# Prompt attention's compressed scores moved apart and cut in column quarters, and four smaller moves, in a one-core hybrid decoder layer

## The chip, the cores and the metric

The kernel runs on one core of one Trainium2 chip. The metric is the device time of one execution, in microseconds; lower is better. Three executions of the kernel before gave 1314.0, 1316.9 and 1320.02 us, so the median is 1316.9 us.

## The reference, cut to what matters

One layer of a decoder, in fp32, for a prompt of 256 tokens and 8 samples of 8 tokens (320 tokens together), with half a feed-forward step on either side:

```
x = x + 0.5 * SwiGLU1(RMSNorm(x))
P = RMSNorm(x) @ w_in_proj           # z, xBC, dt | q, k/v x 3, gates | merge gates
y_ssd = mamba_mixer(z, xBC, dt, ...)      # causal conv, chunked scan, gated norm
y_nsa = gates[0] * o_c + gates[1] * o_s + gates[2] * o_w
x = x + (sig(gA) * (y_ssd @ w_branch_ssm) + sig(gB) * (y_nsa @ w_branch_attn)) @ w_out
x = x + 0.5 * SwiGLU2(RMSNorm(x))
```

`o_c` is attention over compressed keys, one for each block of 32 rows; `o_s` over the 16 best of the blocks of 64 rows, where the ranks come from the sums of the compressed probabilities; `o_w` over a window of 512. For the prompt all blocks fit among the 16, so only the samples rank. Sample queries also see a cache of 2048 rows in pages. The change touches the prompt's part of `o_c`, the samples' ranks, the loads ahead of the samples' attention, and the evacuations behind two of the last projections.

## The kernel before, in words

**Dense stream.** All big products go through `dense()`: an fp32 weight block of 128x1024 is loaded by SyncE (`w_load`, L308), split by ScalarE into a rounded part `wh` (`w_hi`, L317) and by VectorE into the rest `wl` (`w_lo`, L326), and for each of 8 chunks TensorE runs three matmuls of 128x128 by 128x320 (L345 to L347). There are three raw buffers, and a new load is asked for behind `w_lo`, which is given out behind the third chunk of a unit. The order of every engine's queue is the order in which the Python code calls.

**Side work.** Attention, the scan and their preparations are Python generators. After each chunk `S.tick()` may run a step of them (`S.step()`), so their instructions stand between the dense ones on each engine. `yield` ends a step, `wait(n)` lets n of them pass, and `S.defer(n, f)` calls f some n dense units later. Two chains run side by side: prompt_attn, then the scan (`ssd`), then sample_attn; and prompt_cmp, values_tok, new_keys, cmp_sample. During the prompt's attention the dense units are those of xBC, each of which also gives a convolution: `taps` (three VectorE operations, L1245, then a tanh on ScalarE, L1246) and `gate` (L1249, L1252).

**PSUM.** Banks are taken in rings by kind: `pd` (3, dense results), `sc` (2), `pt` (2), `po` (1). A matmul into a bank waits until the bank's last use has been read out.

**The places the change touches.** `values_tok` turns the values over in two halves t (L1035, L1041). In prompt_attn, for each quarter qc of 64 queries, `build` (GpSimd, L1281) writes the queries of a pair of heads into a zeroed matrix, `cmp_a` multiplies it with the compressed keys `kTp` (8 matmuls, L1288) and runs a softmax on VectorE and ScalarE (L1293 to L1303), and `cmp_b` turns four heads of the result (L1310) and copies them out by ScalarE (L1311). The 32 pairs of scores go through `scores` (L1317, L1323, L1326), `norm` (L1334, L1337), `transposes` (L1349, L1350) and `values` (L1366). In `cmp_sample` two matrices U of 30x30 comparisons are made by VectorE (L1169), masked by GpSimd (L1170) and summed by VectorE (L1174, L1175). `early_bias` has SyncE load the samples' bias in 16 pieces (L1440) and the window mask `wb` (L1444), between two stages; sample_attn adds the two first (L1458). Behind the last steps stand the loop over `wbs` (the mixer's branch, `split` of yh and yl), the loop over `wba` and the loop over `wo` (out projection, L2070 to L2076), whose results x are scaled and split again (`norm_pre`: L416 on VectorE, L261 on ScalarE, L264 on VectorE) for the second feed-forward step.

Of the kernel before, what the change touches and what calls it, by code (L numbers as in the profile page):

```python
# [10 lines left out]
F32 = mybir.dt.float32  # L11
# [4 lines left out]
ALU = mybir.AluOpType  # L16
# [91 lines left out]
NST = 2  # L108
# [83 lines left out]
def wait(n):  # L192
    for _ in range(n):
        yield
# [3 lines left out]
def step_kernel(ctx, tc, I, O):  # L198
# [3 lines left out]
    S = Sched()  # L202
# [828 lines left out]
    def values_tok():  # L1031
        for t in range(2):
            pv = bank("pt")
            for i in range(4):
                pe.transpose(pv[:, 128 * i : 128 * i + 128], vr[:, i, 128 * t : 128 * t + 128], ident)  # L1035
            a.copy(flat(vtp[:, t]), pv)
            yield
        pv = bank("pt", (128, 256))
        for br in range(2):
            for h2 in range(2):  # L1040
                pe.matmul(pv[64 * br : 64 * br + 64, 128 * h2 : 128 * h2 + 128], vr[:, 2 * br + h2, 256:], ident,  # L1041
                          start=True, stop=True)
        a.copy(vst, pv)
        yield
# [85 lines left out]
    def cmp_sample():  # L1130
# [35 lines left out]
        for j in range(2):  # L1166
            sj = ib[:, j, 1:31].unsqueeze(1).to_broadcast([128, 30, 30])
            si = ib[:, j, 1:31].unsqueeze(2).to_broadcast([128, 30, 30])
            v.tensor_tensor(U[j], sj, si, op=ALU.is_gt)  # L1169
            g.tensor_tensor(U[j], U[j], um, op=ALU.mult)  # L1170
        yield from wait(4)
        cs = pq.tile([128, 2, 30], F32, name="rkc")
        for j in range(2):
            v.reduce_sum(rk[:, j, :], U[j], axis=AX.X)  # L1174
            v.reduce_sum(cs[:, j, :], U[j].rearrange("p i j -> p j i"), axis=AX.X)  # L1175
            yield from wait(2)
        v.tensor_tensor(rk, rk, cs, op=ALU.subtract)
# [83 lines left out]
    def prompt_attn():  # L1261
# [22 lines left out]
        def cmp_a(qc):  # L1284
            nb, k0 = 2 * (qc + 1), 192 - 64 * qc
            pc = bank("pt", (128, 8, 8))
            for u in range(8):
                pe.matmul(pc[:, u, :nb], qbp[qc % 2][:, u, :], kTp[:, u // 4, :nb], start=True, stop=True)  # L1288
            sc = pl.tile([128, 8, 8], F32, tag="psc", name="psc")
# [84 lines left out]
        build(0)  # L1374
        yield from wait(2)
        cmp_a(0)
        yield from wait(4)
        cmp_b(0, 0)
        cmp_b(0, 1)
        for i in range(4):  # L1380
            scores(i)
            yield
            if i:
                norm(i - 1)
        transposes(0)
        yield
        for i in range(32):
# [10 lines left out]
            if qc < 3:  # L1398
                if u == 1:
                    build(qc + 1)  # L1400
                elif u == 2:
                    cmp_a(qc + 1)
                elif u == 4:
                    cmp_b(qc + 1, 0)
                    cmp_b(qc + 1, 1)
            yield
# [26 lines left out]
    def early_bias(n):  # L1433
        pl = right.enter_context(tc.tile_pool(name="sb", bufs=1, side="right"))
        st["bias"] = pl.tile([128, PAST], F32, name="bias")
        for i in range(2 * T):
            t, s = divmod(i, 2)
# [3 lines left out]
            if i % n == n - 1:  # L1441
                yield
        st["wb"] = pl.tile([128, 8], F32, name="wb")
        sp.dma_start(st["wb"], I["wm"])  # L1444
        yield

# [587 lines left out]
    for h in range(2):  # L2034
# [4 lines left out]
        for k in range(8):  # L2039
            split(yh[:, k, :], yl[:, k, :], xbc[:, 8 * h + k, :])  # L2040
        for _ in range(NST):
            S.step()
        for m in range(8):
# [26 lines left out]
    for m in range(8):  # L2070
        p = bank("pd", (128, NT))
        dense(wo[m], mh, ml, p)
        v.scalar_tensor_tensor(x2[:, m, :], p, 0.5, x2[:, m, :], op0=ALU.mult, op1=ALU.add)  # L2073
        norm_pre(x2, m, P_N2, hh, hl)
        sq.add(x2[:, m, :])
    rsb = norm_scale(sq, so)  # L2076
# [157 lines left out]
```

## Time and profile before

| what | before |
|---|---|
| median of 3 executions | 1316.9 us |
| the profiled execution, its time | 1319.28 us |
| its span (first to last instruction) | 1317.6 us |
| mean granted TensorE clock | 0.981 |
| TensorE busy with matmuls | 1260.2 us (96%) |
| VectorE busy | 877.1 us (67%) |
| ScalarE busy | 590.5 us (45%) |
| GpSimd busy | 347.0 us (26%) |

The span is 1.7 us shorter than the execution's time. Busy times are of the whole span. The stages by the clock of the span: first feed-forward step up to 360 us; projections for attention 375 to 460; xBC with the prompt's attention beside it 460 to 660; merge gates, z and the scan 660 to 830; the samples' attention 840 to 996; wba and wo 1023 to 1076; second feed-forward step to the end. A granted clock of 1 is TensorE's upper level of 2.4 GHz, 0.5 the lower one of 1.2 GHz.

### The profile page before, as it was taken

The numbers are of one execution on the slowest core, as the hardware profiler recorded it, in microseconds if no ns is written. First come the engines' busy times: TensorE is split into PE (matmuls) and PEld (weight loads), VectorE is DVE, ScalarE is ACT, GpSimd is POOL, SyncE is SP. The second block draws the span as 40 slices with busy tenths as digits, with TensorE's granted clock in tenths as the row PEclk, the third lists the DMA queues.
The fourth block names the chain that finished last, engine by engine and source line by source line (L and its number), as shares of the span: only waits on it lengthen the run. The fifth ranks groups of instructions, "written<-read, shape, count | busy, mean of one in ns | idle before, by whom it ended". The sixth has DMA issues, their size and how long they took to land. (4 is left out here: it accounts for less than half of the span.)

```text
span 1317.6 us, 28585 instructions
## 1 busy us (share of the span) xinstructions
PE 1260.2 (96%) x10779; PEld 1151.3 (87%) x10779; DVE 877.1 (67%) x1872; ACT 590.5 (45%) x1149; POOL 347.0 (26%) x567
## 2 busy tenths in 40 slices
PE   8999999999999998889999998898999999999998
PEld 8999999999988888777897777775769999999998
DVE  5576666655586577976568888777678665656542
ACT  4444444444455334446664442455564343333322
POOL 2233221232200335655335664121210010000000
PEclk9899999999999998999999999898999999999999
DMA  8466666766663445521167876998974444444553
GB/s 275 146 215 213 206 197 197 233 202 221 203 195 121 138 147 212 189 69 50 65 207 236 269 228 194 325 339 289 331 284 154 152 145 135 146 154 150 153 163 92
DMA packets 102212, 251.67 MB, mean 191 GB/s; under 512 B 14648, under 2 KB 41273, under 8 KB 100121
## 3 DMA queue, kind: packets, MB, share of 16 engines
q1 hardware_dynamic: 89722, 213.44, 49.1%
q0 software_dynamic: 12352, 36.40, 8.4%
q8 instruction: 85, 1.39, 0.4%
q14 instruction: 53, 0.43, 0.1%
HBM read 235.07 MB, written 23.10 MB: 196 GB/s over the span
## 5 line engine op out<-in xcount | busy, mean ns | idle before, releaser
L345 PE MATMUL ps_pd<-hh,wh 128*128 128x320 f32 x1320 | 440.9, 334 | 2.9 <-ACT hh L261 1.8
L326 DVE TENSOR_TENSOR wl<-wraw,wh 128x1024 fp32r<-128x1024 f32 (+1 forms) x245 | 303.2, 1239 | 178.0 <-ACT wh L317 172.2
L346 PE MATMUL ps_pd<-hl,wh 128*128 128x320 f32 x1320 | 413.8, 314 | 1.3 <-DVE hl L454 1.1
L347 PE MATMUL ps_pd<-hh,wl 128*128 128x320 f32 x1320 | 413.7, 313 | 1.2 <-DVE wl L326 1.1
L317 ACT CAST wh<-wraw 128x1024 fp32r<-128x1024 f32 (+1 forms) x245 | 252.1, 1031 | 139.1 <-PE ps_pd L346 99.8
L345 PEld LDWEIGHTS ps_pd<-hh,wh 128*128 128x128 f32 x1320 | 253.2, 192 | 22.0 <-issue 11.4
L346 PEld LDWEIGHTS ps_pd<-hl,wh 128*128 128x128 f32 x1320 | 253.6, 192 | 9.5 <-issue 4.8
L347 PEld LDWEIGHTS ps_pd<-hh,wl 128*128 128x128 f32 x1320 | 253.0, 192 | 2.0 <-DVE wl L326 2.0
L345 PE MATMUL ps_pd<-ah,wh 128*128 128x320 f32 x352 | 109.4, 311 | 0.0
L347 PE MATMUL ps_pd<-ah,wl 128*128 128x320 f32 x352 | 108.9, 309 | 0.0
L580 DVE TENSOR_TENSOR pgl<-pg,pgh 128x512 fp32r<-128x512 f32 x128 | 82.5, 685 | 29.6 <-ACT pgh L573 29.3
L346 PE MATMUL ps_pd<-al,wh 128*128 128x320 f32 x320 | 98.8, 309 | 0.0
L568 POOL DMA_DIRECT2D pg<-in_cache x136 | 74.2, 546 | 83.6 <-DVE pgl L580 42.3
L238 POOL TENSOR_SCALAR ah<-ff 128x320 fp32r<-128x320 f32 x44 | 20.1, 457 | 275.0 <-DVE ff L482 275.0
L477 ACT ACTIVATE sg<-sg 128x320 f32<-128x320 f32 x44 | 20.8, 472 | 127.1 <-DVE sg L476 127.1
L573 ACT CAST pgh<-pg 128x512 fp32r<-128x512 f32 x128 | 72.7, 616 | 10.0 <-PE ps_sc L714 8.0
L713 PE MATMUL ps_sc<-pgh,w1h 128*128 128x256 f32 x256 | 68.5, 288 | 1.3 <-ACT pgh L573 1.3
L714 PE MATMUL ps_sc<-pgh,w1l 128*128 128x256 f32 x256 | 68.2, 288 | 0.0
L345 PEld LDWEIGHTS ps_pd<-ah,wh 128*128 128x128 f32 x352 | 66.2, 188 | 0.4
L347 PEld LDWEIGHTS ps_pd<-ah,wl 128*128 128x128 f32 x352 | 66.1, 188 | 0.0
L346 PEld LDWEIGHTS ps_pd<-al,wh 128*128 128x128 f32 x320 | 60.2, 188 | 0.0
L1431 POOL DMA_DIRECT2D KV<-in_cache x54 | 29.1, 539 | 109.4 <-PE ps_po L1526 90.6
(476 smaller groups left out, 2207.5 us busy)
## 6 DMA issues: line engine op xcount, KB each, us to landing
wraw<-in_wproj SPq DMA_DIRECT2D x77, 512.0 KB
wraw<-in_w1in SPq DMA_DIRECT2D x44, 512.0 KB
wraw<-in_w2in SPq DMA_DIRECT2D x44, 512.0 KB
pg<-in_cache POOLq DMA_DIRECT2D x136, 128.0 KB, 4.0
pg<-in_cache SPq DMA_DIRECT2D x120, 128.0 KB
KV<-in_cache POOLq DMA_DIRECT2D x54, 256.0 KB, 5.9
KV<-in_cache SPq DMA_DIRECT2D x54, 256.0 KB
wraw<-in_w1out SPq DMA_DIRECT2D x16, 512.0 KB
```

Source lines behind the costliest of these rows:

```text
L317: a.copy(h[:, :n], st["raw"][i][:, :n])
L326: v.tensor_tensor(l[:, :n], st["raw"].pop(i)[:, :n], st["hl"][i][0][:, :n], op=ALU.subtract)
L345: pe.matmul(out, wh[:, s], xh[:, kk, :], start=kk == 0, stop=False)
L346: pe.matmul(out, wh[:, s], xl[:, kk, :], start=False, stop=False)
L347: pe.matmul(out, wl[:, s], xh[:, kk, :], start=False, stop=kk == K - 1)
L477: a.activation(s, s, AF.Silu)
L568: e.dma_start(page(s, half)[:, i, :], I["cache"][ds(r, 1), :, 256 * c : 256 * c + 256].rearrange("o p f -> p (o f)"))
L573: a.copy(h[:, 8 * half : 8 * half + 8, :], page(s, half)[:, :, 64 * q : 64 * q + 64])
L580: v.tensor_tensor(l[:, 8 * half : 8 * half + 8, :], page(s, half)[:, :, 64 * q : 64 * q + 64], h[:, 8 * half : 8 * half + 8, :], op=ALU.su ...
L713: pe.matmul(ph, wh[:, j, :], h[:, :, j, :], start=q + j == 0, stop=False)
L714: pe.matmul(ph, wl[:, j, :], h[:, :, j, :], start=False, stop=False)
L1431: e.dma_start(t[:, j, :], I["cache"][ds(r, 1), :, 512:1024].rearrange("o p f -> p (o f)"))
```

## The change

Six edits:

1. `values_tok` takes a bank of kind `sc` in its second half, for the turns of L1035.
2. In prompt_attn, `cmp_a(0)` stands two steps later than it did, and the two `cmp_b(0, .)` stand behind the first four `scores`, in two steps. In the loop over 32 pairs `build` stands at u = 0 (was 1), `cmp_a` at 3 (was 2), and the halves of `cmp_b` at 5 and 6 (were both at 4).
3. Each of `cmp_a`'s 8 matmuls is cut into 4, for 32 columns of queries each.
4. In `cmp_sample` the comparisons, masks and sums of U are spread over more steps (10 in place of 8 in this stretch).
5. `early_bias` asks for `wb` first, and has one step fewer.
6. In the loop over `wbs` two side steps stand between the splits, behind k = 1 and 4, in place of all `NST` of them behind the last; in the loop over `wo` the evacuation of m = 0 to 6 is put off by 1.5 units.

```diff
     def values_tok():
         for t in range(2):
-            pv = bank("pt")
+            pv = bank("sc" if t else "pt")
@@ cmp_sample
             v.tensor_tensor(U[j], sj, si, op=ALU.is_gt)
+            yield
             g.tensor_tensor(U[j], U[j], um, op=ALU.mult)
-        yield from wait(4)
+            yield from wait(2)
         for j in range(2):
             v.reduce_sum(rk[:, j, :], U[j], axis=AX.X)
+            yield
             v.reduce_sum(cs[:, j, :], U[j].rearrange("p i j -> p j i"), axis=AX.X)
-            yield from wait(2)
+            yield
@@ cmp_a
             for u in range(8):
-                pe.matmul(pc[:, u, :nb], qbp[qc % 2][:, u, :], kTp[:, u // 4, :nb], start=True, stop=True)
+                for c in range(4):
+                    o = slice(32 * c, 32 * c + 32)
+                    pe.matmul(pc[o, u, :nb], qbp[qc % 2][:, u, o], kTp[:, u // 4, :nb], start=True, stop=True)
@@ prompt_attn
         build(0)
-        yield from wait(2)
+        yield from wait(4)
         cmp_a(0)
-        yield from wait(4)
-        cmp_b(0, 0)
-        cmp_b(0, 1)
+        yield
         for i in range(4):
             scores(i)
             yield
             if i:
                 norm(i - 1)
+        cmp_b(0, 0)
+        yield
+        cmp_b(0, 1)
         transposes(0)
@@
             if qc < 3:
-                if u == 1:
+                if u == 0:
                     build(qc + 1)
-                elif u == 2:
+                elif u == 3:
                     cmp_a(qc + 1)
-                elif u == 4:
-                    cmp_b(qc + 1, 0)
-                    cmp_b(qc + 1, 1)
+                elif u in (5, 6):
+                    cmp_b(qc + 1, u - 5)
@@ early_bias
+        st["wb"] = pl.tile([128, 8], F32, name="wb")
+        sp.dma_start(st["wb"], I["wm"])
         for i in range(2 * T):
...
-        st["wb"] = pl.tile([128, 8], F32, name="wb")
-        sp.dma_start(st["wb"], I["wm"])
-        yield
@@ loop over wbs
             split(yh[:, k, :], yl[:, k, :], xbc[:, 8 * h + k, :])
-        for _ in range(NST):
-            S.step()
+            if k in (1, 4):
+                S.step()
@@ loop over wo
         dense(wo[m], mh, ml, p)
-        v.scalar_tensor_tensor(x2[:, m, :], p, 0.5, x2[:, m, :], op0=ALU.mult, op1=ALU.add)
-        norm_pre(x2, m, P_N2, hh, hl)
-        sq.add(x2[:, m, :])
+        def evac(m=m, p=p):
+            v.scalar_tensor_tensor(x2[:, m, :], p, 0.5, x2[:, m, :], op0=ALU.mult, op1=ALU.add)
+            norm_pre(x2, m, P_N2, hh, hl)
+            sq.add(x2[:, m, :])
+        if m < 7:
+            S.defer(1.5, evac)
+        else:
+            evac()
```

**On TensorE, around the first quarter's `cmp_b`.** Before, the eight turns (L1310) stand together between dense chunks, right ahead of the first of the `scores` (L1317):

```order
L347 MATMUL ps_pd<-hh,wl 128x320
L1310 MATMUL ps_pt<-con,psc 2x128 x8
L1317 MATMUL ps_sc<-knp,blob 128x2x64
L345 MATMUL ps_pd<-hh,wh 128x320
```

After the change they are L1314, in two fours, with chunks and the samples' compressed scores (L1139) between them, and the first turns of the prompt's scores (L1353, the L1349 of before) follow the second four:

```order
L347 MATMUL ps_pd<-hh,wl 128x320
L1314 MATMUL ps_pt<-con,psc 2x128 x4
L345 MATMUL ps_pd<-hh,wh 128x320
L346 MATMUL ps_pd<-hl,wh 128x320
L347 MATMUL ps_pd<-hh,wl 128x320
L1139 MATMUL ps_sc<-kcv,qbs 64x64 x16
L345 MATMUL ps_pd<-hh,wh 128x320
L346 MATMUL ps_pd<-hl,wh 128x320
L347 MATMUL ps_pd<-hh,wl 128x320
L1314 MATMUL ps_pt<-con,psc 2x128 x4
L1353 MATMUL ps_pt<-con,pS 128x128 x2
```

The four `scores` that stood behind the eight turns now stand ahead of all these rows.

**On VectorE, around the second quarter's `cmp_a`.** Before, both comparisons U (L1169) stand right ahead of its softmax (L1293 to L1303), and a convolution's gate (L1249) follows:

```order
L1169 TENSOR_TENSOR U<-ib 128x900 x2
L1293 TENSOR_TENSOR psc<-ps_pt,pb 128x8x4
L1294 TENSOR_REDUCE psm<-psc 128x8
L1295 TENSOR_SCALAR psm<-psm 128x8
L1296 TENSOR_TENSOR psc<-psc,psm 128x8x4
L1298 TENSOR_REDUCE psm<-psc 128x8
```

After it one comparison stands a gate, a norm and two scores earlier, ahead of a weight split (L326) and a convolution's taps (L1247, the L1245 of before); the other follows the softmax (not shown):

```order
L1169 TENSOR_TENSOR U<-ib 128x900
L1251 SCALAR_TENSOR_TENSOR xbc<-cvt,cvo 128x256
L1254 SCALAR_TENSOR_TENSOR xbc<-cvt,cvo 128x64
L1338 RECIPROCAL pm<-pm 128x2
L1327 ISA pS,pm<-ps_sc,pb 128x64
L1327 ISA pm 128x1
L1327 ISA pS,pm<-ps_sc,pb 128x64
L1327 ISA pm 128x1
L326 TENSOR_TENSOR wl<-wraw,wh 128x1024
L1247 SCALAR_TENSOR_TENSOR cvo<-pr_4945,cwh,cvo 128x344 x3
L1297 TENSOR_TENSOR psc<-ps_pt,pb 128x8x4
L1298 TENSOR_REDUCE psm<-psc 128x8
```

The softmax of `cmp_a` (from L1297 on) now follows a split and taps, and one of the comparisons comes ahead of them.

**On SyncE, at the end of the scan.** `out_ssmS` are writes of the scan's states, `bias` the samples' bias, `wb` the window mask. Before:

```order
L1440 DMA bias<-trev 16x2x512 x4
L1733 DMA out_ssmS<-h_9644 128x512
L1733 DMA out_ssmS<-h_9652 128x512
L308 DMA wraw<-in_wproj 128x1024
L1440 DMA bias<-trev 16x2x512 x2
L1444 DMA wb<-in_wm 128x8
L308 DMA wraw<-in_wproj 128x1024
```

After:

```order
L1446 DMA bias<-trev 16x2x512 x4
L308 DMA wraw<-in_wproj 128x1024
L1736 DMA out_ssmS<-h_9761 128x512
L1736 DMA out_ssmS<-h_9769 128x512
L1446 DMA bias<-trev 16x2x512 x2
L308 DMA wraw<-in_wproj 128x1024
```

The mask is gone from here (it stands in front of the first piece of the bias), and the weight load that stood behind two state writes now stands ahead of them, so that those writes are between it and the last two pieces of the bias.

## Rows read from the trace of the kernel before

**Rows 1.** The page's first part: busy time, share of the span and instructions of each engine.

```profile
PE 1260.2 (96%) x10779; PEld 1151.3 (87%) x10779; DVE 877.1 (67%) x1872; ACT 590.5 (45%) x1149; POOL 347.0 (26%) x567
```

**Rows 2.** Busy time of each engine in two stretches of the prompt's attention: the stretch, its length, then for PE, PEld, DVE, ACT and POOL the busy us (and instructions), the granted clock, the DMA share and GB/s.

```profile
480.00:600.00 120.00, 100.33 (x1006) 90.18 (x1004) 94.76 (x248) 52.80 (x163) 72.47 (x130) 0.94 0.43 151
540.00:560.00 20.00, 16.32 (x125) 14.65 (x123) 19.19 (x42) 9.48 (x34) 13.12 (x23) 0.91 0.42 155
```

**Rows 3.** TensorE's timeline in the same stretch, the rows with the long waits and one between them: start, duration, operation, result from operands, tile, count, and in brackets the idle time before it and what ended that.

```profile
490.29 0.66 PE L1035 MATMUL ps_pt<-con,vr 128*128 128x128 f32 x4 [2.58 <-DVE kTp L1127]
491.76 0.67 PE L1041 MATMUL ps_pt<-con,vr 128*64 128x128 f32 x8
502.00 2.84 PE L1288 MATMUL ps_pt<-kTp,blob 128*128 128x2 f32 x16 [2.37 <-POOL blob L1281]
537.67 1.95 PE L1288 MATMUL ps_pt<-kTp,blob 128*128 128x4 f32 x16 [2.03 <-POOL blob L1281]
551.89 0.60 PE L1310 MATMUL ps_pt<-con,psc 128*4 128x128 f32 x4 [2.96 <-ACT pT L1350]
554.54 0.41 PE L1349 MATMUL ps_pt<-con,pS 128*128 128x128 f32 x2 [0.73 <-ACT blob L1311]
570.92 0.57 PE L1366 MATMUL ps_po<-pT,vtp 128*64 128x64 f32 x8 [3.59 <-ACT qn L1370]
```

**Rows 4.** What let those matmuls go: VectorE's copy of `kTp`, and GpSimd's clearing (L1267) and writing (L1281) of the query matrix, from the timelines of these engines.

```profile
490.07 0.16 DVE L1127 COPY kTp<-ps_pt 128x16 f32<-128x16 f32 x1
496.81 3.52 POOL L1267 MEMSET blob<- 128x4096 f32 x1
500.42 1.53 POOL L1281 TENSOR_SCALAR blob<-qn 64x512 f32<-64x512 f32 x2
535.45 2.17 POOL L1281 TENSOR_SCALAR blob<-qn 64x512 f32<-64x512 f32 x2
```

**Rows 5.** Four stretches in which the granted clock (third figure from the end) is low; columns as in rows 2.

```profile
502.00:510.00 8.00, 8.00 (x37) 7.96 (x38) 5.45 (x16) 2.03 (x5) 2.93 (x5) 0.57 0.14 37
540.00:544.00 4.00, 4.00 (x20) 3.96 (x19) 3.90 (x6) 0.92 (x5) 4.00 (x4) 0.57 0.06 20
834.00:842.00 8.00, 7.09 (x39) 5.52 (x39) 5.05 (x21) 1.52 (x3) 2.15 (x4) 0.58 1.04 404
1082.00:1088.00 6.00, 6.00 (x34) 5.97 (x33) 4.53 (x17) 1.40 (x2) 0.00 (x0) 0.72 0.53 174
```

**Rows 6.** ScalarE's timeline around the wait of 551.89: the convolution's tanh, the copy of the turned scores behind it, and the copy that `cmp_b` makes.

```profile
551.09 0.49 ACT L1246 ACTIVATE cvt<-cvo 128x344 f32<-128x344 f32 x1 [2.27 <-DVE pm L1334]
551.49 0.35 ACT L1350 COPY pT<-ps_pt 128x256 f32<-128x256 f32 x1
553.83 1.04 ACT L1311 COPY blob<-ps_pt 4x512 f32<-4x512 f32 x2
```

**Rows 7.** The comparisons U and `cmp_a`'s small operations on VectorE, and the masking of U on GpSimd, from the two timelines.

```profile
541.93 0.19 DVE L1294 TENSOR_REDUCE psm<-psc 128x8 f32<-128x32 f32 x1
542.46 1.87 DVE L1296 TENSOR_TENSOR psc<-psc,psm 128x32 f32<-128x32 f32 x1
544.85 1.34 DVE L1299 TENSOR_SCALAR psm<-psm 128x8 f32<-128x8 f32 x1
542.37 3.80 POOL L1170 TENSOR_TENSOR U<-U,blob 128x900 bf16<-128x900 bf16 x2
```

**Rows 8.** TensorE's timeline: `cmp_a` at the upper clock without a wait, and groups of small matmuls on 64 or 32 columns.

```profile
583.42 1.95 PE L1288 MATMUL ps_pt<-kTp,blob 128*128 128x6 f32 x16
494.31 2.04 PE L1053 MATMUL ps_sc<-ksm,qbs 128*64 128x8 f32 x64
531.54 0.43 PE L1157 MATMUL ps_pt<-cs__6551,con 128*32 128x64 f32 x16
910.33 0.65 PE L1526 MATMUL ps_po<-KV,sT 128*32 128x64 f32 x32
```

**Rows 9.** The end of the scan: SyncE's timeline, the piece of the chain that ended last, and the VectorE and TensorE rows that waited.

```profile
815.75 1.00 SPq L1733 DMA_DIRECT2D out_ssmS<-h  x2
822.40 1.18 SPq L1440 DMA_DIRECT2D bias<-trev  x2
823.63 8.43 DMA wb<-in_wm
832.14 0.17 DVE L1458 TENSOR_TENSOR wb<-wb,bias 128x8 f32<-128x8 f32 x1 [3.01 <-DMA wb<-in_wm]
834.91 1.29 PE L396 MATMUL ps_pt<-ones,sqa 128*128 128x1 f32 x6 [3.63 <-DVE ncol L401]
```

**Rows 10.** TensorE's wait in the mixer's branch, and the piece of the chain that ended last with the page that it waited for.

```profile
900.93 1.02 PE L1481 MATMUL ps_sc<-xbc,qbs 64*32 64x512 f32 x2 [2.53 <-DVE yl L264]
895.30 7.76 DMA KV<-in_cache
```

**Rows 11.** The end of the wo loop: VectorE's split of a weight and the x of m = 7 behind it, ScalarE's cast of the last chunk, and TensorE's wait for it.

```profile
1078.10 1.23 DVE L326 TENSOR_TENSOR wl<-wraw,wh 128x1024 fp32r<-128x1024 f32 x1 [0.82 <-ACT wh L317]
1079.25 0.48 DVE L2073 SCALAR_TENSOR_TENSOR x<-ps_pd,x 128x320 f32<-128x320 f32 x1
1080.18 0.46 ACT L261 CAST hh<-hf 128x320 fp32r<-128x320 f32 x1 [2.11 <-DVE hf L416]
1080.70 0.41 PE L345 MATMUL ps_pd<-hh,wh 128*128 128x320 f32 x1 [1.82 <-ACT hh L261]
```

## The prediction

> **What bounds the kernel now.** The first part of the page says TensorE is busy 96% of the span [rows 1], so what can be won is its idle time, 1317.6 less 1260.2, about 57 us, and the time that it runs at its lower clock. I therefore read the busy times by stretches of 20 us first, then TensorE's timeline with its waits in the stretches that are not full, then the timelines of the engine each wait names, and the granted clock in stretches of 2 us. Idle time gathers in one place: from 480 to 600, beside the prompt's attention, TensorE is busy 100.33 of 120 us [rows 2]. VectorE is busy 94.76 us there, and in the worst 20 us 19.19 [rows 2]: in this stage it is close to being the bound itself. The rest is a wait at the end of the scan, one in the samples' attention and one behind the out projection [rows 9 to 11].
>
> **A, the bank of the values' turns.** The turns at 490.29 waited 2.58 us for VectorE's copy of kTp [rows 3], since kTp stood in the same ring `pt`; the copy took 0.16 us at 490.07 [rows 4], late because it stands behind convolution work in VectorE's queue. In a bank of kind `sc` they need not wait. But the ring `pt` goes on: the next user, the product of L1041, now gets kTp's bank. Before, it started 1.47 us behind those turns (491.76 less 490.29). Without the wait the turns start at 487.71, so TensorE stands at L1041 at 489.2 and waits until 490.2. Of 2.58, 1.0 or 1.1 stays. I take -1.5 (bounds 0, if what follows waits instead, and -2.6).
>
> **B, the compressed scores.** Two of the long waits are for GpSimd's writing of the query matrix: 2.37 us at 502.00 and 2.03 at 537.67 [rows 3]. In the first, GpSimd clears the matrix for 3.52 us from 496.81 and writes it until 501.95; in the second it writes from 535.45 for 2.17 us, and `cmp_a` is one pair behind [rows 4]. The change puts five chunks of dense work (two of them and the four turns fill A's 1.47 us, so about half a microsecond each) ahead of the first `cmp_a`, just what it waited, and two more pairs between `build` and the others. I count both waits as gone: -4.4. Behind each the clock fell to the lower level: 8 us at 0.57 and 4 us at 0.57 [rows 5], which lost 8 x 0.43 + 4 x 0.43 = 5.2. If the waits go, these go: -5.2. Both together: bounds 0 (the waits return a few rows later) and -9.6.
>
> The waits of 2.96 us at 551.89 and 0.73 at 554.54, at the second half of `cmp_b` and the turns behind it, have another cause. ScalarE's copy of earlier turns (551.49) stands behind the tanh of a convolution (551.09), and that waited for VectorE [rows 6]; the bank is not free before the copy. Setting the halves a step apart lets the first half's bank be read out in time, but each half, on its own, still takes a bank that ScalarE must have emptied, and a tanh may stand in front as before. I count 0 here (bounds -3.7, and a loss, below). At the first quarter a new wait appears: the first turns of scores come right behind the second half of `cmp_b`, into the bank of the first half, whose copy now stands behind a tanh. A copy of this size costs 0.5 us (1.04 for two, [rows 6]); copy and tanh (0.49) together come to 1.0. So +1.0 (bounds 0 and 3.0, the longest wait of the kind, [rows 3]).
>
> The spread of U changes no work. VectorE's small operations took 1.87 and 1.34 us while GpSimd masked U for 3.80 us, where one of their kind took 0.19 [rows 7]; some 2.7 us of VectorE come from that overlap. Now one masking lies beside taps and a split, which it can stretch as well. Cover is TensorE's own dense work; I count 0 (bounds -2.7, and +2.0 if the steps that are added push work into a busier place).
>
> Not all of this can stay won. With 16 us out of these 120, VectorE's 94.76 would lie in 104, a share of 91%, and in the 20 us where it was at 96% TensorE idled 3.7 [rows 2]. I let one fall of the clock come back, at the price of the smaller one above: +1.7. The wait of 3.59 us at 570.92, behind ranks and taps [rows 3], I leave as it is.
>
> **C, quarters.** One `cmp_a` without a wait takes 1.95 us for 16 instructions [rows 8]. With quarters there are 64. The trace has no 128-row matmul of 32 columns on so few columns; the nearest rows are 0.65 us for 32 (20 ns each), 0.43 for 16 (27) and 2.04 for 64 (32) [rows 8]. These give 1.3, 1.7 and 2.04 us. I take 1.7, from the row with 32 columns beside the same stage: four times -0.25, -1.0 (bounds +0.4 and -2.6). The Trainium skill, TensorEngine Tiling (Array Packing), section Performance Considerations, puts a fixed cost of about 60 cycles on each matmul, so that 64 would take 1.6 us, as an estimate at 2.4 GHz; its Overview gives a 4x speedup for a dimension of 32, which would be 0.49. No run here shows the second; it is the last rival.
>
> **D, the mask first.** The pass of TensorE's wait at 834.91 goes back over VectorE to the add of `wb` and bias, which waited 3.01 us for `wb`, issued last at 823.63 and 8.43 us under way [rows 9], at full DMA load (share 1.04, [rows 5]). Asked first, `wb` is long there. But the last two pieces of the bias were issued only 1.2 us before it (822.40 for 1.18, [rows 9]) into the same queues, and the order shows two state writes now ahead of them (1.00 us of SyncE, [rows 9]). If they take as long, the wait gets shorter by 0.2; if the writes are ready, by up to 1.2. I take -0.4 (bounds -6.4, the 3.0 us and the 3.4 us of the clock at 834, [rows 5], and +3.0, as much again as the wait now: the page loads start a step earlier and share full queues with the bias).
>
> **E, the branch's splits.** The wait at 900.93 names a split, but a page under way for 7.76 us ends the chain there [rows 10]. TensorE's order is as before, only VectorE's and ScalarE's changes. So 0 (bounds -2.5 and, if a step's own VectorE work delays the last split, +1.5).
>
> **F, the out projection.** For m = 7, x stood behind a weight's split of 1.23 us, and the cast of its chunk at 1080.18 ended a wait of 1.82 [rows 11]. With the others put off, x of m = 6 comes behind that split and x of m = 7 right behind the split of m = 6; the cast then waits for the chain of m = 6 (x 0.48, the cast 0.46, [rows 11], and two more of that size) in place of 1.23. The loop before it starts earlier, by one evacuation. Stepping both queues by hand, I get the last cast 0.4 to 1.4 us earlier: -0.9 (bounds 0 and -3.5, with the clock behind it: 6 us at 0.72, 1.7, [rows 5]).
>
> **The sum.** -1.5 (A) -4.4 -5.2 +1.0 +1.7 (B) -1.0 (C) -0.4 (D) -0.9 (F) = -10.7. The profiled execution took 1319.28 us, 1.7 above its span, and 2.4 above the median of 1316.9. So 1308.6 beside the first, 1306.2 beside the second: **1306**.
>
> **Rivals.**
> 1. *The waits only move.* VectorE is the bound of the stage; what TensorE gains on GpSimd it loses to tanh and taps some rows on. For it: VectorE's 96% [rows 2], and that the waits of 551.89 and 570.92 are of this kind. Against it: over the 120 us VectorE is at 79%. Then only C, F and one fall of the clock stay: -1.0 -0.9 -1.7 = -3.6, 1313.3.
> 2. *The whole stage clears up.* The new wait doesn't come, no fall of the clock returns, the 3.7 us of 551.89 and 554.54 go, and A gives its 2.6: -10.7 -1.0 -1.7 -3.7 -1.1 = -18.2, 1298.7. For it: the waits come where copies of several kinds meet in one step, and these are pulled apart. Against it: ScalarE's order still has a tanh that waits for VectorE.
> 3. *Halves that each wait, slower.* `cmp_b` now asks for a bank at eight separate places. If each waits as the one at 551.89 did (2.96 us, [rows 3]), the loss is 8 x 2.96 = 23.7 in place of my 1.0: +12.0, 1328.9. It decides from the fifth on: four waits are 11.8, as much as the sum gives without the 1.0. Against it: in the trace before, third and fourth quarters show no such wait at the same turns.
> 4. *Quarters side by side.* If four quarters, on columns of their own, ran at once, 64 would cost what 4 of 16 do now, 0.49 us: four times -1.46, 5.8 in place of 1.0, and 1301.4. Against it: the small groups of [rows 8] come at 20 to 32 ns, one behind the other.
>
> **How the numbers follow.** Forecast 0.48, rival 1 0.24, rival 2 0.15, rival 3 0.07, rival 4 0.06. The forecast's own range is 1300 to 1311: D and E at their bounds, or a fall of the clock more or less. A measurement tells 0.5% (6.6 us) from no change, so faster is below 1310.3 and slower above 1323.5. Faster: nearly all of the forecast (0.45) and rivals 2 and 4, 0.66. Same: the rest of the forecast and rival 1, and the milder half of rival 3, 0.28. Slower: 0.06. For 8 times in 10 the range takes in rivals 2 (partly), 4 and 1 with bounds: 1297 to 1316.
>
> **What would show it.** A: turns of the values without a wait, the product behind them with one of 1 us. B: `cmp_a` without a wait for GpSimd, and a granted clock of 1.00 in the 20 us from 500; a wait of about 1 us at the first turns of scores. C: the 64 pieces in 1.3 to 2.0 us. D: the add of `wb` waiting for bias, by under 3 us. E: the wait for a page as before. F: a wait under 1 us behind the out projection. Wrong I would be if TensorE's busy share between 480 and 600 stayed at 84%, with waits on ScalarE and VectorE in place of GpSimd, or if the clock fell as often at other places.

## The result, and the profile after

The changed kernel takes 1308.8 us (median of 7, 1305.9 to 1313.3), the kernel before 1318.4 (7 runs, where 1316.9 was the median of three): a ratio of 0.9924, 95% interval 0.9900 to 0.9948. The forecast of 1306 was 2.8 us low; its sum of -10.7 us stands against -9.6 measured. But the sum came out right over terms that did not: the stage on which most of it rested got no fuller.

The first part of the page after, and five stretches by engine (columns as in [rows 2]):

```profile
PE 1260.2 (96%) x10971; PEld 1150.4 (88%) x10971; DVE 879.9 (67%) x1872; ACT 589.4 (45%) x1149; POOL 340.2 (26%) x567
480.00:600.00 120.00, 99.21 (x1100) 88.67 (x1099) 97.66 (x260) 52.66 (x163) 69.17 (x129) 0.91 0.42 149
502.00:510.00 8.00, 6.84 (x104) 6.35 (x105) 6.09 (x15) 2.12 (x5) 5.37 (x8) 1.00 0.58 204
500.00:520.00 20.00, 13.77 (x135) 12.19 (x133) 17.01 (x54) 6.87 (x25) 11.65 (x19) 0.84 0.65 237
514.00:522.00 8.00, 6.55 (x147) 5.82 (x148) 6.35 (x29) 5.04 (x22) 3.72 (x11) 0.61 0.55 199
558.00:566.00 8.00, 6.26 (x37) 5.53 (x38) 7.93 (x20) 4.44 (x15) 4.00 (x8) 0.59 0.66 236
```

Where [rows 2] had TensorE busy 100.33 of 120 us, with a clock of 0.94, it is now 99.21 with 0.91. The fall of the clock at 502 is gone ([rows 5] had 0.57), and others have come: 0.61 from 514 and 0.59 from 558, behind the two long waits shown next. (This profiled execution was the slowest of the seven, 1313.3 us; the same waits stand in the second profile, below.)

TensorE's timeline shows what became of the waits of [rows 3]:

```profile
490.89 0.60 PE L1035 MATMUL ps_sc<-con,vr 128*128 128x128 f32 x4
493.64 0.66 PE L1041 MATMUL ps_pt<-con,vr 128*64 128x128 f32 x8 [1.27 <-DVE kTp L1127]
503.16 0.33 PE L1067 MATMUL ps_sc<-con,ts 128*128 128x128 f32 x1 [1.22 <-ACT ts L1062]
505.18 0.85 PE L1292 MATMUL ps_pt<-kTp,blob 128*32 128x2 f32 x64
515.45 0.77 PE L1321 MATMUL ps_sc<-knp,blob 128*128 128x128 f32 x2 [5.01 <-DVE pm L1327]
542.17 0.72 PE L1292 MATMUL ps_pt<-kTp,blob 128*32 128x4 f32 x64
550.80 0.60 PE L1314 MATMUL ps_pt<-con,psc 128*4 128x128 f32 x4
559.74 0.66 PE L1353 MATMUL ps_pt<-con,pS 128*128 128x128 f32 x2 [7.02 <-ACT pT L1354]
587.79 1.25 PE L1196 MATMUL ps_sc<-con,mb 128*32 128x128 f32 x8 [2.84 <-DVE msk L1197]
```

The turns of the values wait no more, and the product behind them waits 1.27 us, as A said. Then 1.22 us come back at the turn of the new keys' scores: A's gain is returned ten microseconds later. `cmp_a` (L1292) waits for GpSimd neither time, as B said, and takes 0.85 and 0.72 us, half or less of the 1.7 that C allowed. But two waits are new, 5.01 us at the third of the prompt's scores and 7.02 us at a pair's turns, more than the 2.37, 2.03 and 2.96 that went.

Both have one picture. For the second, VectorE, GpSimd and ScalarE ahead of 559.74:

```profile
543.43 1.55 DVE L326 TENSOR_TENSOR wl<-wraw,wh 128x1024 fp32r<-128x1024 f32 x1 [0.63 <-ACT wh L317]
543.88 2.88 POOL L1171 TENSOR_TENSOR U<-U,blob 128x900 bf16<-128x900 bf16 x1
544.91 3.48 DVE L1247 SCALAR_TENSOR_TENSOR cvo<-pr,cwh,cvo 128x344 f32<-128x344 f32 x3
554.06 1.90 POOL L1171 TENSOR_TENSOR U<-U,blob 128x900 bf16<-128x900 bf16 x1
554.11 2.93 DVE L326 TENSOR_TENSOR wl<-wraw,wh 128x1024 fp32r<-128x1024 f32 x1 [1.53 <-ACT wh L317]
556.96 1.79 DVE L1247 SCALAR_TENSOR_TENSOR cvo<-pr,cwh,cvo 128x344 f32<-128x344 f32 x3
558.84 0.49 ACT L1248 ACTIVATE cvt<-cvo 128x344 f32<-128x344 f32 x1 [4.76 <-DVE pm L1338]
559.24 0.35 ACT L1354 COPY pT<-ps_pt 128x256 f32<-128x256 f32 x1
```

Read it backwards. The turns wait for the copy at 559.24, which stands behind a tanh (L1248), which waits for taps (the trace names `pm`, the small operation right behind them in VectorE's queue), which wait for a weight's split (L326), before which VectorE stood idle 1.53 us for ScalarE's part of the weight. That split takes 2.93 us where the next has 1.2, and starts within 0.05 us of GpSimd's mask of U. The other mask lies under taps of 3.48 us, where undisturbed ones take 1.79. How much of the wait this makes is seen in mask_dve, below. For the wait of 5.01 the same holds with GpSimd's product of the new keys' scores (L1072):

```profile
509.10 2.16 POOL L1072 TENSOR_TENSOR blob<-tpT,con 128x1024 f32<-128x1024 f32 x1 [1.53 <-DVE tpT L1069]
508.94 3.31 DVE L1247 SCALAR_TENSOR_TENSOR cvo<-pr,cwh,cvo 128x344 f32<-128x344 f32 x3
514.94 0.21 DVE L1327 CUSTOM_DVE_ANT_0 pS<-ps_sc,pb 128x64 f32<-128x64 f32 x1
```

Between taps and the scores' softmax at 514.94 stand `cmp_a`'s nine small operations, now ahead of the first scores in VectorE's queue: the bank of the first scores is read out late, and the third waits. (How much of the 5.01 is the lengthened taps was not tried.)

At the end of the scan the add of mask and bias, and the last pieces of the bias, against [rows 9]:

```profile
820.37 0.86 SPq L1736 DMA_DIRECT2D out_ssmS<-h  x2
821.28 2.15 SPq L1446 DMA_DIRECT2D bias<-trev  x2
822.21 6.64 DMA bias<-trev
829.65 0.17 DVE L1461 TENSOR_TENSOR wb<-wb,bias 128x8 f32<-128x8 f32 x1 [0.80 <-issue]
832.43 0.78 PE L396 MATMUL ps_pt<-ones,sqa 128*128 128x1 f32 x6 [2.06 <-DVE ncol L401]
```

It is the bias that lands last now, 6.64 us under way, and TensorE's wait is 2.06 in place of 3.63 (2.82 in the second profile). Behind the out projection, against [rows 11]:

```profile
1075.72 0.46 ACT L261 CAST hh<-hf 128x320 fp32r<-128x320 f32 x1 [1.23 <-DVE hf L416]
1076.23 0.42 PE L345 MATMUL ps_pd<-hh,wh 128*128 128x320 f32 x1 [0.97 <-ACT hh L261]
```

The wait is 0.97 for 1.82.

### The profile page after: what moved, and what is told of

Read it like the earlier page. It is cut to its first block, busy times and chain, and to the rows that moved or that the text cites. A ratio compares the mean times of both kernels' runs of the same rounds, so it can differ in the third digit from the quotient of the medians.

```text
span 1311.6 us, 28962 instructions
## 1 busy us (share of the span) xinstructions
PE 1260.2 (96%) x10971; PEld 1150.4 (88%) x10971; DVE 879.9 (67%) x1872; ACT 589.4 (45%) x1149; POOL 340.2 (26%) x567
## 4 chain that ended last, share of the span: by engine, by line
PE 64%; DVE 11%; issue 11%; DMA 5%; ACT 4%; POOL 3%; SPq 1%; POOLq 1%; DVEq 0%; ACTq 0%
PE ps_pd L345 17%; PE ps_pd L346 15%; PE ps_pd L347 15%; DVE wl L326 3%; PE ps_sc L1484 2%; PE ps_po L1529 2%; DVE cvo L1247 1%; ACT wh L317 1%; PE ps_sc L713 1%; PE ps_sc L714 1%; PE ps_sc L723 1%; PE ps_po L1370 1%; PE ps_pt L1515 1%; PE ps_sc L1321 1%; DMA ecb<-ascr 1%
## 5 line engine op out<-in xcount | busy, mean ns | idle before, releaser
L326 DVE TENSOR_TENSOR wl<-wraw,wh 128x1024 fp32r<-128x1024 f32 (+1 forms) x245 | 305.5, 1249 | 184.6 <-ACT wh L317 180.6
```

The costliest lines, as they stand in the source:

```text
L326: v.tensor_tensor(l[:, :n], st["raw"].pop(i)[:, :n], st["hl"][i][0][:, :n], op=ALU.subtract)
```

## The experiments

Medians are compared between kernels measured together on one chip; ratios are to the kernel before, measured beside them. For "where", four stretches are cut at the same weight splits (L326, the 93rd, 113th, 141st, 161st and last of 245) in VectorE's timeline: prompt attention, scan, samples' attention, rest. The two cuts of the first for the kernel before and after:

```profile
480.64 1.21 DVE L326 TENSOR_TENSOR wl<-wraw,wh 128x1024 fp32r<-128x1024 f32 x1
645.53 1.22 DVE L326 TENSOR_TENSOR wl<-wraw,wh 128x1024 fp32r<-128x1024 f32 x1
```

```profile
483.99 1.21 DVE L326 TENSOR_TENSOR wl<-wraw,wh 128x1024 fp32r<-128x1024 f32 x1
644.09 1.22 DVE L326 TENSOR_TENSOR wl<-wraw,wh 128x1024 fp32r<-128x1024 f32 x1
```

| kernel | median us (n) | ratio, 95% interval | prompt attention | scan | samples | rest |
|---|---|---|---|---|---|---|
| before | 1318.4 (7) | | 164.9 | 194.2 | 169.4 | 296.0 |
| changed | 1308.8 (7) | 0.9924, 0.9900 to 0.9948 | 160.1 | 192.6 | 169.8 | 292.7 |
| after_again | 1310.4 (12) | 0.9943, 0.9918 to 0.9968 | 162.9 | 192.6 | 170.2 | 292.7 |
| undo_B | 1311.9 (12) | 0.9941, 0.9922 to 0.9959 | 160.1 | 191.4 | 168.3 | 292.7 |
| undo_U | 1327.2 (10) | 1.0086, 1.0054 to 1.0118 | 160.9 | 198.0 | 178.4 | 293.7 |
| undo_C | 1316.0 (12) | 0.9971, 0.9949 to 0.9994 | 163.6 | 193.4 | 177.1 | 294.2 |
| undo_D | 1313.4 (8) | 0.9966, 0.9938 to 0.9993 | 161.1 | 195.3 | 176.1 | 293.3 |
| undo_F | 1310.4 (7) | 0.9935, 0.9910 to 0.9959 | 158.9 | 192.6 | 167.9 | 294.8 |
| undo_A | 1309.5 (6) | 0.9932, 0.9907 to 0.9957 | 157.5 | 191.6 | 171.5 | 294.2 |
| undo_E | 1307.4 (6) | 0.9918, 0.9890 to 0.9945 | 157.5 | 190.4 | 171.0 | 292.7 |
| undo_U_steps | 1310.6 (12) | 0.9930, 0.9902 to 0.9957 | 156.0 | 192.6 | 172.1 | 294.2 |
| mask_dve | 1308.0 (7) | 0.9913, 0.9883 to 0.9942 | 158.2 | 193.9 | 171.6 | 292.7 |
| only_C | 1317.8 (12) | 1.0004, 0.9976 to 1.0031 | 161.7 | 194.7 | 171.2 | 297.3 |
| D_steps | 1312.5 (12) | 0.9949, 0.9927 to 0.9970 | 157.5 | 189.7 | 173.3 | 293.3 |

A stretch is of one profile. How wide it scatters is seen where the code up to it is the same: changed, after_again, undo_D, undo_F, undo_E and D_steps have the same prompt attention, and 157.5 to 162.9 us (mean 159.7). Three profiles are of executions far from their kernel's median: undo_C (1324.5 us, the slowest of 12) and undo_D (1320.4) are 7 to 8 us above it, undo_B (1303.9, the fastest of 12) is 8 below.

**The changed kernel again (after_again).**

> The changed kernel once more, on the chip of the next three, so that each can be held against it, and for a second profile: the profiled execution was the slowest of seven (1313.3 us against a median of 1308.8) and showed TensorE waits of 5.0 us (third scores of the prompt, for VectorE) and 7.0 us (turns of the scores, for ScalarE). If these two waits belong to the order of the queues, they stand in this profile too, at the same instructions and within 1 us; if they come from how this one execution fell, one of them is under 2 us here. Time 1305 to 1313.

```profile
509.39 0.77 PE L1321 MATMUL ps_sc<-knp,blob 128*128 128x128 f32 x2 [5.01 <-DVE pm L1327]
556.43 0.66 PE L1353 MATMUL ps_pt<-con,pS 128*128 128x128 f32 x2 [7.00 <-ACT pT L1354]
```

TensorE's timeline in the second profile has both waits, to 0.02 us: they belong to the order of the queues. What lies between the two profiled executions (1313.3 and 1310.5 us) is not in them.

**The places of the compressed scores undone (undo_B).**

```diff
-        yield from wait(4)
+        yield from wait(2)
         cmp_a(0)
-        yield
+        yield from wait(4)
+        cmp_b(0, 0)
+        cmp_b(0, 1)
@@ (and the two cmp_b behind the scores taken out; in the loop)
-                if u == 0:
+                if u == 1:
                     build(qc + 1)
-                elif u == 3:
+                elif u == 2:
```

> The changed kernel with the places of build, cmp_a and cmp_b in prompt_attn as before (the quarters stay). By the prediction's sum the move is worth 4.4 + 5.2 - 1.0 - 1.7 = 6.9 us, so this is 6.9 slower than the changed kernel (about 1315.5), with the two waits for GpSimd back at 2.0 to 2.4 us each. The rival, that waits only move: the move is worth 0 to 2 us, since the profile of the changed kernel shows 5.0 and 7.0 us of waits that it did not have before; then this is at 1308 to 1311.

1311.9 against 1310.4 for the changed kernel beside it, ratios 0.9941 and 0.9943: nothing that can be measured, where 6.9 us were forecast. TensorE's timeline of this kernel:

```profile
497.71 0.23 PE L1292 MATMUL ps_pt<-kTp,blob 128*32 128x2 f32 x4 [2.99 <-POOL blob L1283]
498.56 1.02 PE L1292 MATMUL ps_pt<-kTp,blob 128*32 128x2 f32 x60 [0.61 <-POOL blob L1283]
544.98 0.60 PE L1314 MATMUL ps_pt<-con,psc 128*4 128x128 f32 x4 [2.85 <-ACT pT L1354]
```

The wait for GpSimd at the first quarter is back, and so is the one for the copy behind the tanh (2.99 and 2.85 us); at the second quarter `cmp_a` waits 1.84 us, for VectorE. 5.01 and 7.00 are gone, though one mask of U stretches a weight split here too (2.92 us), and the prompt attention takes 160.1 us, close to the mean of the others. The move exchanges waits of equal worth: rival 1, for this part.

**The spread of the ranks undone (undo_U), and undone with the count of steps kept (undo_U_steps).** The two differ by two empty steps behind the sums.

```diff
             v.tensor_tensor(U[j], sj, si, op=ALU.is_gt)
-            yield
             g.tensor_tensor(U[j], U[j], um, op=ALU.mult)
-            yield from wait(2)
+        yield from wait(4)
@@ (the sums: one wait(2) behind each pair; in undo_U_steps one more wait(2) at the end)
```

> The changed kernel with the comparisons of the samples' ranks back in their old steps. The prediction counted their spread at 0: then this is within 2 us of the changed kernel. The rival: the first masking on GpSimd (2.88 us) now lies beside the taps of a convolution (3.48 us in place of 1.8) and the second (1.90) beside a weight split (2.93 in place of 1.23), and both are in the chain that ends the 7.0 us wait; then the spread costs 3 us or more, this is at 1303 to 1306, and the 7.0 us wait is below 3.5 here.

> As undo_U (comparisons, masks and sums of the ranks in their old steps), with two empty steps behind them, so that the count of steps is the changed kernel's ten. Undone with the count of eight, the kernel lost 17 us, but its trace lost them in the samples' attention, 370 us later, and none between 480 and 645. Theory of the count: the two chains take turns, so two steps fewer put everything behind into other chunks, and the loss is the samples' page loads meeting other waits; then this is within 3 us of the changed kernel (1308 to 1313). Theory of the spread: the work itself, in its old steps, collides; then this is at 1320 or more.

Without the two steps the kernel is 1327.2 us, 16.9 slower than the changed one beside it and slower than before; with them 1310.6. So where the comparisons stand is worth nothing that shows, and how many steps they take is worth some 17 us in this kernel. Neither theory ahead of undo_U had that; its 7.0 us wait gave way to two of 3.83 and 2.75, and the kernel lost all the same. The loss is not in the prompt attention (160.9) but later, 5 us in the scan and 8 in the samples' attention. Busy time from 940 to 1000, undo_U and then undo_U_steps:

```profile
940.00:1000.00 60.00, 54.29 (x742) 37.16 (x741) 32.94 (x131) 29.39 (x71) 7.52 (x14) 0.89 0.70 244
```

```profile
940.00:1000.00 60.00, 59.25 (x874) 45.88 (x868) 44.51 (x172) 33.10 (x76) 7.55 (x14) 1.00 0.65 234
```

The two chains take turns, so two steps fewer in one move what stands behind against the other by two turns. Two of TensorE's waits in undo_U, in the scan and in the samples' attention:

```profile
802.71 0.80 PE L1839 MATMUL ps_sc<-xh,bz 128*128 128x512 f32 x1 [3.35 <-DVE h L1841]
955.96 1.03 PE L1482 MATMUL ps_sc<-xbc,qbs 64*32 64x512 f32 x1 [3.69 <-DMA xbc<-in_cache]
```

The second is for a page, and the clock behind it is 0.57 (955 to 963). The first shows the count by itself: the three kernels with eight steps (before, only_C, undo_U) wait 2.3 to 3.4 us at that place and take 194.2 to 198.0 us for the scan, the eleven with ten wait 1.2 us there and take 189.7 to 195.3. But the kernel before has eight steps too and is some 8 us faster than undo_U: the price of the count hangs on the other edits.

**The quarters undone (undo_C), and alone (only_C).**

```diff
-                for c in range(4):
-                    o = slice(32 * c, 32 * c + 32)
-                    pe.matmul(pc[o, u, :nb], qbp[qc % 2][:, u, o], kTp[:, u // 4, :nb], start=True, stop=True)
+                pe.matmul(pc[:, u, :nb], qbp[qc % 2][:, u, :], kTp[:, u // 4, :nb], start=True, stop=True)
```

> The changed kernel with cmp_a's 8 matmuls whole again in place of 32 quarters. The prediction: quarters save 0.25 us each time, 1.0 us in all, so this is 1 us slower than the changed kernel (1309.8). The rival, from the profile after, where the 64 instructions took 0.85 and 1.04 us in place of 1.95: they save 0.9 to 1.1 us four times, about 4 us, so this is at 1312 to 1313.

> The kernel before with nothing but cmp_a's matmuls cut into quarters. The prediction's term: 1.0 us faster than before. The term as the profile after has it: 64 instructions in 0.85 to 1.04 us in place of 1.95 at the upper clock, four times, and 0.9 more where the clock was low: 4 to 5 us faster than before, a ratio of 0.996 to 0.997.

Undone: 1316.0 against 1310.4 beside it, 5.7 us slower. The first and the third of its four groups:

```profile
503.28 1.95 PE L1290 MATMUL ps_pt<-kTp,blob 128*128 128x2 f32 x16
587.70 3.58 PE L1290 MATMUL ps_pt<-kTp,blob 128*128 128x6 f32 x16
```

The third ran at the lower clock (0.50); the other three take 1.95 us each. In the changed kernel the four take 0.85, 0.72, 1.04 (also at 0.50) and 0.72, so the matmuls themselves are 6.1 us longer. The prompt attention takes 163.6 us against the mean of 159.7, 3.9 more, which is just outside the scatter. The samples' attention is longer too (177.1); since this profile is of the slowest execution, how the 5.7 divides isn't read from it. Alone, on the kernel before: a ratio of 1.0004, no change, although its prompt attention is 3.2 us shorter (161.7 for 164.9, less than the scatter). The interval (0.9976 to 1.0031) holds 3 us less only at its edge: what the quarters give alone is not settled by time.

**The mask asked last again (undo_D), and asked first with the step kept (D_steps).** The second has an empty `yield` behind the bias.

```diff
-        st["wb"] = pl.tile([128, 8], F32, name="wb")
-        sp.dma_start(st["wb"], I["wm"])
         for i in range(2 * T):
@@
+        st["wb"] = pl.tile([128, 8], F32, name="wb")
+        sp.dma_start(st["wb"], I["wm"])
+        yield
```

> The changed kernel with the window mask asked last again. The prediction gave 0.4 us to asking first: then this is within 1 us of the changed kernel, and TensorE's wait behind the add of mask and bias (3.63 us before) is at most 0.5 us longer here. The rival: the whole wait and the fall of the clock behind it come from the mask's landing, up to 3.0 + 3.4 us; the profile after has no wait at that place, and then this is 4 to 6 us slower, with the wait back at 2 us or more and the clock at its lower level behind it.

> The changed kernel with one empty step behind the bias, so that the mask is still asked first but the first page loads come as late as in the kernel before. Undoing this edit cost about 3 us (undo_D). If that was the mask's landing, this is within 1.5 us of the changed kernel and the add of mask and bias waits under 2 us. If it was the step count, so that page loads meet the samples' attention at another point, this is 2.5 us or more slower than the changed kernel (1312 and up), with the loss behind 890 as in undo_D.

undo_D: 1313.4, a ratio of 0.9966 against 0.9924 and 0.9943 of the changed kernel, some 3 to 5 us. D_steps: 0.9949, between them, and within the intervals of undo_D and of after_again. VectorE's add and TensorE's waits, undo_D and then D_steps:

```profile
829.90 0.17 DVE L1462 TENSOR_TENSOR wb<-wb,bias 128x8 f32<-128x8 f32 x1 [4.10 <-DMA KV<-in_cache]
831.81 1.29 PE L396 MATMUL ps_pt<-ones,sqa 128*128 128x1 f32 x6 [5.41 <-DVE ncol L401]
898.93 1.96 PE L1485 MATMUL ps_sc<-KV,qbs 64*32 64x512 f32 x14 [4.28 <-DMA KV<-in_cache]
```

```profile
821.60 0.17 DVE L1462 TENSOR_TENSOR wb<-wb,bias 128x8 f32<-128x8 f32 x1 [0.39 <-DMA wraw<-in_wproj]
890.80 1.96 PE L1485 MATMUL ps_sc<-KV,qbs 64*32 64x512 f32 x14 [5.02 <-DMA KV<-in_cache]
```

The add waits 4.10 us in undo_D and 0.39 in D_steps. With the mask first it waits 0.4 to 1.8 us in ten profiles and 3.30 in one (mask_dve), with the mask last 1.85 to 4.10 in three; the 4.10 the trace puts to a page's load, asked for behind the mask, and not to the mask. With the page loads a step later, TensorE waits 4 to 5 us for a page around 895, in both kernels, where the changed one waits 2.2. The kernels without that step wait at most 2.6 us there, but for undo_C with 3.96; the kernel before, which has the step, waits 2.53 for a split and then 1.24 for a page. So the edit has two parts, and only one was in the prediction. That either of them pays in time is not shown.

**The out projection, the values' bank and the branch undone (undo_F, undo_A, undo_E).** Each is the edit of the same name taken back from the diff of the change.

> The changed kernel with the evacuations of the out projection put back ahead of the next unit. The prediction gave 0.9 us: the wait behind the out projection is back at 1.8 us from 0.97, and this is 0.9 slower. The rival: the clock's fall behind the wait goes with it, and this is 2.5 us slower; the granted clock then shows it in the 6 us behind the wait.

> The changed kernel with the second half of the values' turns in the old kind of bank. The prediction gave 1.5 us: the turns wait 2.6 us again in place of 1.27 at the product behind them, and this is 1.3 to 1.5 slower. The rival: VectorE and GpSimd are late anyway for what follows (the profile after has a new wait of 1.22 at the turn of the new keys' scores), so that the wait goes back into that one, and this is within 0.5 us of the changed kernel.

> The changed kernel with the side steps of the mixer's branch behind all eight splits again. The prediction gave 0, since a page's load ends the wait there: this is within 1 us of the changed kernel, with the two waits at the first scores of the third sample as in its profile (0.3 us and none). The rival: the splits did hold TensorE, and the 2.5 us wait of the kernel before comes back with a fall of the clock behind it, so 2.5 to 5 us slower.

All three are within the noise of the changed kernel (0.9935, 0.9932, 0.9918). undo_F's wait behind the out projection is 1.84 us, 0.87 longer, as forecast. The clock from 1.3 us behind the start of the matmul that waited, in undo_F and in the changed kernel:

```profile
1071.10:1077.10 6.00, 6.00 (x34) 5.97 (x33) 4.52 (x17) 1.44 (x2) 0.00 (x0) 0.72 0.50 175
1077.50:1083.50 6.00, 6.00 (x44) 5.97 (x43) 5.45 (x18) 1.99 (x2) 0.00 (x0) 1.00 0.54 168
```

0.72 is what [rows 5] had there. All three kernels without the edit show a fall of the clock, and a last stretch of 294.8 us or more. Of the eleven with it, eight show none, and 292.7 to 293.7 us; three (undo_A, undo_C, undo_U_steps) show 0.72 behind a wait of 0.97, and 294.2. So the fall costs some 0.5 to 1.5 us there, beside the 0.87 of the wait, and with the edit it is rarer but not ruled out. undo_A's turns wait 2.57 us again, and the 1.22 at the new keys' scores is gone: the rival, that the wait goes back. In undo_E the wait of 2.5 us did not come back, nor a fall of the clock at that place: its splits held nothing.

**The masks of U on VectorE (mask_dve).**

```diff
-            g.tensor_tensor(U[j], U[j], um, op=ALU.mult)
+            v.tensor_tensor(U[j], U[j], um, op=ALU.mult)
```

> The changed kernel with the two masks of U (L1171) made by VectorE in place of GpSimd, the same product. Theory: TensorE's wait of 7.0 us at the turns of the scores comes from GpSimd's masks stretching VectorE's work beside them (taps 3.49 us in place of 1.8, a weight split 2.92 in place of 1.23, together 3.4 us). Then taps and split are back at 1.8 and 1.2 us, VectorE pays some 0.6 to 1.1 us for each mask, the wait falls to 3 to 5.5 us, and the kernel gains 1 to 4 us. Rival: the masks aren't what stretches them, and VectorE, which is the bound, gets 1 to 2 us more: the wait grows to 8 us or more, the kernel is 1 to 2 us slower.

VectorE's first mask, the taps and the split that the masks had stretched, and TensorE's wait:

```profile
539.38 1.08 DVE L1171 TENSOR_TENSOR U<-U,blob 128x900 bf16<-128x900 bf16 x1
542.85 1.96 DVE L1247 SCALAR_TENSOR_TENSOR cvo<-pr,cwh,cvo 128x344 f32<-128x344 f32 x3 [0.89 <-POOL cvo L1243]
550.53 1.23 DVE L326 TENSOR_TENSOR wl<-wraw,wh 128x1024 fp32r<-128x1024 f32 x1 [0.53 <-ACT wh L317]
555.09 0.66 PE L1353 MATMUL ps_pt<-con,pS 128*128 128x128 f32 x2 [5.95 <-ACT pT L1354]
```

Split and taps are back at 1.23 and 1.96 us: GpSimd's masks did stretch them. But the masks cost VectorE 1.08 us each, so that 2.2 us of masks stand in its queue for 3.2 of stretching; the wait is 5.95, 1.1 shorter and a little above the forecast. The rest of the 7.0 is the queue's order and length. 1308.0 us can't be told from the changed kernel's.

## Why the prediction was right, and where its steps were wrong

**The sum.** -10.7 against -9.6 us, the sign and the size. By what each undoing cost, though, the terms were others: C some 4 to 6 us (forecast 1.0), D some 3 to 5 (0.4), B between 0 and 2 (6.9), A, E and F nothing that can be measured (1.5, 0, 0.9). B gave some 5 to 7 us less than forecast, C and D together some 6 to 10 more: the misses cancelled, and the agreement of the sum was luck. These are prices of undoing in the changed kernel, not shares of the 9.6: C alone, on the kernel before, gave nothing that shows, and undoing U's spread cost 17. The shares are not resolved. By the stretches (one profile of the kernel before) the prompt attention gave 5 us (164.9 to 159.7, the mean of six), the scan 1.6, the rest 3.3, and the samples' attention none.

**B, the step that failed.** "I count both waits as gone" was right, and the clock's fall at 502 is gone too. What was wrong is to count the other end as one new wait of 1.0 us. The new order put `cmp_a`'s softmax ahead of the scores in VectorE's queue and U's masks beside taps and a split, and 5.0 and 7.0 us came. The wait that I forecast is there (0.83 to 0.84 us at L1353, in every profile that has the new order but after_again). The prediction had the facts: VectorE at 96% in the worst stretch, and small operations of 1.87 us under a mask of 3.80 [rows 7]. It put the spread of U at 0 and noted that the masks could stretch a split and taps "as well", without asking who waits for those: a tanh, a copy behind it, a bank. Rival 1 (0.24) named the mechanism; it was right for this edit, and the total was carried by others. The tests that the prediction set itself came out against it: the busy share, which was not to stay at 84%, is 83%, with waits on ScalarE and VectorE in place of GpSimd, and the clock over the 20 us from 500, which was to be 1.00, is 0.84.

**C, mis-sized.** The mechanism was right, the price not: 0.72 to 0.85 us for 64 instructions at the upper clock, where I had 1.7 and a lower bound of 1.3 from rows with 20 ns for each. They come at 11 to 13 ns. The rows with 32 columns that gave 1.3 and 1.7 have 64 moving columns, where these have 2 to 8; they too go around four column groups in the code, so that it isn't the groups that set them apart. What does was not tried. Rival 4's 0.49 us was nearer than the forecast. Of the two places in the Trainium skill (TensorEngine Tiling (Array Packing)), the speedup of up to 4x of its Overview is nearer than the fixed cost of Performance Considerations, by which 64 would take 1.6 us, as an estimate. Measured are 2.3 to 2.7 times (1.95 us to 0.85 and 0.72).

**D, one part unseen.** The bias landing in the mask's place was as forecast (a wait of 0.4 to 1.8 us at the add in place of 3.0, but for 3.3 in mask_dve). Left out was the step that the edit takes away: I named it only as a danger ("the page loads start a step earlier"), but with the step put back TensorE waits longer for a page around 890. How the 3 to 5 us that undoing D costs divide is open.

**The count of steps, a term that the sum did not have.** U's spread adds two steps, at a price of 0 in the prediction, "+2.0 if the steps that are added push work into a busier place". With eight steps in place of ten the same kernel loses 17 us. That the changed kernel has a good count was luck of the forecast, not its working.

**A, E, F.** A: the 1.27 us at the product was forecast as 1.0 to 1.1; that the rest comes back at the next wait was its bound 0. E: 0, as forecast. F: 0.85 us in the wait, as forecast; the fall of the clock behind it, which was only in the bound, is gone as well in the changed kernel's profile.

## What to carry to other kernels

In a stage where one engine is nearly always busy (VectorE here, at 96% of the worst 20 us), the price of moving an operation is not the wait that it leaves but the queue that it joins: list, for each instruction that now stands behind it, who waits for that one. Where side work is dealt out by a count of steps, a step more or fewer is an edit of its own; undo an edit once with the count kept and once without. Undo each part of a change alone even when the total agrees with the forecast, since wrong terms can add up to the right sum; and try a part by itself as well, since undoing it (C: 5.7 us) and having it alone (none) need not agree.

## What the runs showed of the hardware

64 matmul instructions of 128 rows by 32 columns on 2 to 8 moving columns take 0.72 to 0.85 us at the upper clock, 11 to 13 ns each, against 32 ns for each of 64 on 64 columns with 8 moving ones [rows 8] and 122 ns for each of 16 on 128 columns, with 2 and with 8 moving ones alike (undo_C). A two-operand product on GpSimd of 1.9 to 2.9 us lengthens VectorE's two-operand operations beside it by 1.5 to 1.7 us, for taps and weight splits alike, and not when VectorE makes the product itself. The two look as if they took turns: the split that starts 0.05 us behind a mask ends 1.08 us behind the mask's end (557.04 and 555.96), where it takes 1.2 alone; and the mask of 2.88 us, which starts while a split runs, ends 1.78 us behind that split (546.76 and 544.98), where the other mask takes 1.90.
